# A decoder step on one core: the last feature pair of each chunk is split in two parts, and the end's pinned steps move one tile later

## The chip, the core and the metric

The kernel runs on one core of one Trainium2 chip. The metric is the device time of one execution in microseconds (us); a smaller time is better. The core has a matrix engine (TensorE, "PE" in the profile; its weight loads are "PEld"), a vector engine (VectorE, "DVE"), a scalar engine (ScalarE, "ACT"), GpSimd ("POOL") and SyncE ("SP"), which here only starts transfers. Each engine works through its own queue in order.

## What is computed

One step of a hybrid decoder trunk with model width 1024 on 520 tokens (512 new ones of a prompt and 8 single ones of a batch), all in float32:

```python
h = h + 0.5 * swiglu(rms_norm(h), ffn1)          # 1024 -> 2816 -> 1024
m = mixer(rms_norm(h))                           # pooling mixer + Mamba-2 mixer
h = h + m
h = h + 0.5 * swiglu(rms_norm(h), ffn2)          # 1024 -> 2816 -> 1024
y = rms_norm(h)
# swiglu(x) = (silu(x @ wg) * (x @ wu)) @ wd
```

The change touches the two feed-forward blocks (FFN1 and FFN2) and the last normalisation.

## The kernel before, in words

**Layout.** Features lie on the 128 partitions, tokens along the row. 520 tokens are two halves of 260 (`HALVES`); 2816 hidden features are 22 tiles of 128. A matrix product in nearly float32 precision is made of three matmuls (`mm3`, lines 121 to 126): each operand is split into a high part in a shorter format and the low remainder, and high x high (L122), high x low (L125) and low x high (L126) are added in one accumulator. So each operand needs a cast by ScalarE (the high part) and then a subtraction by VectorE (the low part).

**Seven products instead of eight.** The FFN class works on 2 x 2 blocks with a scheme of the Strassen-Winograd kind: `product` (L336) makes products number 1 to 7 of a step. Their left sides are sums of weight blocks, which `load` (L310) builds after the DMA (tiles `raw`, then `s`, `whi`, `wlo`, `shi`, `slo`); their right sides are seven sums of the activations, called slots 0 to 6, each with a high and a low part. For gate and up the slots of the normalised input lie in `xth` and `xtl`. For the down projection they are made of a *pair* of hidden features by `g_split` (L247): from the gated features `gx` (first of the pair) and `go` (second), each with two halves, it makes four differences `xd` (tile `gd` in the profile: L257, L258, L259, L261), and from these seven operands `x` the tile `gt`: slots 0 to 6 hold the high parts (casts on ScalarE, L265), slots 7 to 13 the low parts (subtractions on VectorE, L266). The tile's slot 0 is `gx[0]`, 1 is `go[0]`, 2 is `go[1]`, 3 to 6 are `xd[0]` to `xd[3]`. Only `go[0]` and `xd[3]` need the half that the closing product 4 gives.

**Order of a step.** `step` (L426) makes product 1 of step k, then product 4 of the step before, which was left pending (`flush`, L400), then products 5, 6, 3, 7, 2 of k, and then `gates` (L368), which on VectorE and ScalarE makes SiLU and the second half of the gated feature (`up(k, 1, ...)`, L383). `close` (L389) makes its first half (`up(k, 0, ...)`, L394) from product 4 and then calls `g_split` (L395).

**Chunks.** The 22 feature tiles fall into chunks of 6, 6, 6 and 4 (`CHUNKS`, L34). `rest` (L406) makes the steps of a chunk, then the first step of the next chunk, and then four down steps (c, 0), (c, 2), (c, 4), (c, 6), each with two tiles of the model width. So the last pair of a chunk closes in the first step of the next chunk, and the down step (c, 0) comes right behind that step. A down step reads three pairs, of which the last one (features 5, 11, 17) is the youngest. There are three such places in each FFN, six in all. The last chunk has no pairs and goes through `down` in FFN1 and `down_by_half` (L471) in FFN2. In the profile the down steps of FFN1 have the tiles `A1d`, `BE1d`, those of FFN2 `A2d`, `BE2d`.

**Who sets the order.** The tile framework's scheduler places the instructions of each engine by its own timeline, with the order of the program text as priority; where `keep_in_program_order` is called, instructions stay in that order among each other ("pinned").

**The end.** `down_by_half` makes for each half of the tokens the eight output tiles d = 0 to 7: twelve matmuls, an addition into `h` (L504), then `after2` (L611): a square on ScalarE, its sum on VectorE (L155), and a scaled copy into `hg` (L629). When tile 0 of the second half is reached, the sum of the first half is complete: `finish(0, ...)` (L631) puts the matmul with ones, two square roots on ScalarE (L639) and a list `todo` of six pinned steps on record: two reciprocals of 130 (L642) and four multiplications that give two output tiles each (L646), each followed by its DMA (L648, on SP's queue). `after2` takes one step of `todo` off per tile of the second half from d = 3 on (L615). With d = 7, `finish(1, ...)` adds the six steps of the second half, and all that is left is made.

Of the kernel before, what the change touches and what calls it, by code (L numbers as in the profile page):

```python
# [9 lines left out]
F32 = mybir.dt.float32  # L10
F32R = mybir.dt.float32r
AF = mybir.ActivationFunctionType
ALU = mybir.AluOpType
# [3 lines left out]
P = 128  # L17
# [4 lines left out]
HB = NT // 2  # L22
# [39 lines left out]
def tile_trunk_step(ctx: ExitStack, tc: tile.TileContext, ins: dict, outs: dict):  # L62
    nc = tc.nc
# [18 lines left out]
    def v(name, i, n=P):  # L82
        return vec[:n, VEC[name] + i : VEC[name] + i + 1]
# [37 lines left out]
    def mm3(ps, whi, wlo, xhi, xlo, start, stop, pin=False, **kw):  # L121
        first = nc.tensor.matmul(ps, whi, xhi, start=start, stop=False, **kw)  # L122
        if pin:
            tc.keep_in_program_order(first)
        nc.tensor.matmul(ps, whi, xlo, start=False, stop=False, **kw)  # L125
        nc.tensor.matmul(ps, wlo, xhi, start=False, stop=stop, **kw)  # L126

    def ws(w, k, m=P):
        return w[:, k * m : (k + 1) * m]
# [18 lines left out]
    def sumsq(acc, d, hs, name):  # L148
        n = hs.stop - hs.start
        if d == 0:  # L150
            nc.scalar.activation(out=acc[:, hs], in_=h[:, d, hs], func=AF.Square)
        else:
            sq = tmp.tile([P, HB], F32, tag="ta", name=f"sq_{name}_{d}")
            nc.scalar.activation(out=sq[:, :n], in_=h[:, d, hs], func=AF.Square)
            nc.vector.tensor_tensor(out=acc[:, hs], in0=acc[:, hs], in1=sq[:, :n], op=ALU.add)  # L155
# [48 lines left out]
    class Ffn:  # L204
# [39 lines left out]
            nc.scalar.copy(g[:, 0], t)  # L244
            nc.vector.tensor_tensor(out=g[:, 1], in0=t, in1=g[:, 0].bitcast(F32), op=ALU.subtract)

        def g_split(self, f):  # L247
            role = self.role(f)
            if role == "plain":
                self.g_plain(f, self.out[f])  # L250
            if role != "second":
                return
            gx, go = self.gx, self.out[f]
            self.gx = None
            t = self.gt[f] = self.gp.tile([P, 14, HB], F32R, tag="gt", bufs=3, name=f"gt{self.i}_{f}")
            xd = self.gp.tile([P, 4, HB], F32, tag="xd", name=f"gd{self.i}_{f}")
            nc.vector.tensor_tensor(out=xd[:, 0], in0=gx[:, 0], in1=gx[:, 1], op=ALU.subtract)  # L257
            nc.vector.tensor_tensor(out=xd[:, 1], in0=go[:, 1], in1=gx[:, 1], op=ALU.subtract)  # L258
            nc.vector.scalar_tensor_tensor(out=xd[:, 2], in0=xd[:, 1], scalar=-1.0, in1=gx[:, 0], op0=ALU.mult,  # L259
                                           op1=ALU.subtract)  # L260
            nc.vector.scalar_tensor_tensor(out=xd[:, 3], in0=xd[:, 2], scalar=-1.0, in1=go[:, 0], op0=ALU.mult,  # L261
                                           op1=ALU.subtract)
            for x, q in ((gx[:, 0], 0), (go, slice(1, 3)), (xd, slice(3, 7))):
                hi, lo = t[:, 0:7][:, q], t[:, 7:14][:, q]
                nc.scalar.copy(hi, x)  # L265
                nc.vector.tensor_tensor(out=lo, in0=x, in1=hi.bitcast(F32), op=ALU.subtract)  # L266

        def plain_load(self, f, j=None):
            if f not in self.raw:
                self.raw[f] = raw_pair(f"{self.i}_{f}")  # L270
            src = ins[f"w{self.i}gu"]
            for u in range(2):
                if j is None:
                    nc.sync.dma_start(out=self.raw[f][:, u], in_=src[2 * f + u])
                    continue
                q = (t.rearrange("p (q c) -> p q c", q=2)[:, :, j * P : j * P + P]
                     for t in (self.raw[f][:, u], src[2 * f + u]))
                nc.sync.dma_start(out=next(q), in_=next(q))
# [57 lines left out]
        def product(self, k, p):  # L336
            if k not in self.A:
                with tc.issue_after(self.behind[k]) if k in self.behind else nullcontext():
                    self.load(k)
                n = f"{self.i}_{k}" if not isinstance(k, tuple) else f"{self.i}d{k[1]}_{k[0]}"  # L340
                self.A[k] = ps[0].tile([P, 512], F32, tag="A", bufs=2, name=f"A{n}")
                self.BE[k] = ps[0].tile([P, 2, 512], F32, tag="BE", bufs=2, name=f"BE{n}")
                self.ac[k] = [self.wx.tile([P, 2, HB], F32, tag="ac", bufs=3, name=f"ac{n}_{q}") for q in range(2)]
            slot, dst, opens = {1: (0, 0, True), 2: (1, 1, True), 5: (3, 2, True), 6: (5, 0, False),
                                3: (2, 2, False), 7: (4, 0, False), 4: (6, 0, False)}[p]
            out = self.A[k] if dst == 0 else self.BE[k][:, dst - 1]
            (whi, wlo), k0 = self.w[k][p]
            xth, xtl = self.nx[:2]
            n = len(self.chunks[k[0]]) // 2 if isinstance(k, tuple) else KD // 2
            for j in range(n):  # L350
                if isinstance(k, tuple):
                    t = self.gt[self.chunks[k[0]][2 * j + 1]]
                    xhi, xlo = t[:, slot], t[:, 7 + slot]
                else:
                    xhi, xlo = xth[:, j, slot], xtl[:, j, slot]
                mm3(out[:, :HB], ws(whi, k0 + j), ws(wlo, k0 + j), xhi, xlo, opens and j == 0,
                    j == n - 1, skip_group_check=True)
            a, c = self.ac[k]
            keep = {1: a[:, 0], 6: a[:, 1], 7: c[:, 0], 5: c[:, 1]}.get(p)
            if keep is not None:  # L360
                nc.scalar.copy(keep, out[:, :HB])  # L361
            if p == 7:
                nc.vector.tensor_tensor(out=c[:, 0], in0=c[:, 0], in1=c[:, 1], op=ALU.add)
# [4 lines left out]
        def gates(self, k):  # L368
            n = f"{self.i}_{k}" if not isinstance(k, tuple) else f"{self.i}d{k[1]}_{k[0]}"
            r = self.nx[3].rearrange("p (b t) -> p b t", b=2)  # L370
            tg = self.tg[k] = self.wx.tile([P, 2, HB], F32, tag="tg", bufs=2, name=f"tg{n}")
            a, c = self.ac[k]
            nc.vector.tensor_tensor(out=tg, in0=self.BE[k][:, :, :HB], in1=a, op=ALU.add)  # L373
            if isinstance(k, tuple):
                hd, hn = h[:, k[1]], h[:, k[1] + 1, HALVES[1]]
                nc.vector.tensor_tensor(out=hd, in0=hd, in1=tg.rearrange("p b t -> p (b t)"), op=ALU.add)
                nc.vector.tensor_tensor(out=hn, in0=hn, in1=c[:, 0], op=ALU.subtract)
                return
            nc.vector.tensor_tensor(out=tg, in0=tg, in1=r, op=ALU.mult)  # L379
            nc.scalar.activation(out=tg, in_=tg, func=AF.Silu)  # L380
            self.g_homes(k)
            nc.vector.tensor_tensor(out=tg, in0=tg, in1=r, op=ALU.mult)  # L382
            self.up(k, 1, c[:, 0])  # L383

        def up(self, k, b, u):
            out, tg = self.out[k][:, b], self.tg[k][:, b]
            nc.vector.scalar_tensor_tensor(out=out, in0=u, scalar=-0.5, in1=tg, op0=ALU.mult, op1=ALU.mult)

        def close(self, k):  # L389
            if isinstance(k, tuple):  # L390
                hn = h[:, k[1] + 1, HALVES[0]]
                nc.vector.tensor_tensor(out=hn, in0=hn, in1=self.A[k][:, :HB], op=ALU.subtract)
                return
            self.up(k, 0, self.A[k][:, :HB])  # L394
            self.g_split(k)  # L395

        def scales(self):
            rstds(self.nx, f"f{self.i}")
# [125 lines left out]
    for j in range(KD // 2):  # L524
        for d in (j, j + KD // 2):
            q = slice(NVEC + d * NT if d else 0, NVEC + (d + 1) * NT)
# [82 lines left out]
    todo, late = [], []  # L609

    def after2(d, b, hs):  # L611
        hg, _, last = res
        if (d, b) == (0, 1):
            finish(0, [last[:, HALVES[0]]])
        elif b and todo and d > 2:  # L615
            todo.pop(0)()
        if b and d >= KD - 2:
            late.append(tmp.tile([P, HB], F32, tag="ta", name=f"sq_last{d}"))
            nc.scalar.activation(out=late[-1], in_=h[:, d, hs], func=AF.Square)
        else:  # L620
            sumsq(last, d, hs, f"l{d}{b}")
        if (d, b) == (KD - 1, 1):
            nc.vector.tensor_scalar(out=hg[:, d, hs], in0=h[:, d, hs], scalar1=v("final_norm", d), scalar2=None,
                                    op0=ALU.mult)
            finish(1, [last[:, hs], *late])
            while todo:
                todo.pop(0)()
            return
        nc.scalar.activation(out=hg[:, d, hs], in_=h[:, d, hs], func=AF.Copy, scale=v("final_norm", d))  # L629
# [585 lines left out]
```

## Time and profile before

| what | value |
|---|---|
| three timed runs | 992.83, 993.07 and 990.26 us; median 992.83 us |
| the profiled execution | 992.07 us, of which 990.3 us are the span of its instructions |
| mean granted TensorE clock in it | 0.996 of full speed |
| moved by DMA | 145.46 MB, mean 147 GB/s |

FFN1 lies from the start to about 360 us, the mixer to about 625 us, FFN2 from there to the end. All times of the trace count from the start of the span. In a timeline row the first number is the start, the second the duration of an instruction, then come engine, line, operation, what it writes and reads, and in brackets the idle time of the engine before it and what ended that. Because the engines are pipelined, an instruction starts a little before the one ahead of it has ended; the distance from start to start is what it takes of the queue.

### The profile page before, as it was taken

What the parts mean: (1) busy time and instruction counts of PE and PEld (TensorE: products, weight loads), DVE (VectorE), ACT (ScalarE), POOL (GpSimd) and SP (SyncE); (2) the same over time, 40 slices, a digit from 0 to 9 for tenths busy, and PEclk for the clock granted to TensorE, in tenths of its full rate; (3) what the DMA queues carried; (4) which work ended last, traced back from release to release, by engine and by line L of the source; (5) the groups of instructions that cost most, each with busy time, mean ns of one, the idle gap of its engine ahead of it and who ended that gap; (6) DMA issues with size and microseconds to landing.
All of it is one profiled execution on the core that took longest, in us unless ns stands there. A gap on an engine that the chain in (4) does not pass through costs nothing.

```text
span 990.3 us, 20220 instructions
## 1 busy us (share of the span) xinstructions
PE 955.2 (96%) x7636; PEld 929.3 (94%) x7636; DVE 877.1 (89%) x1612; ACT 677.7 (68%) x1251; POOL 218.2 (22%) x319
## 2 busy tenths in 40 slices
PE   7999999999999999999999999999999999999995
PEld 6899999999999999999899998899999989998995
DVE  7998999889989698788979987999989988997976
ACT  7676777677767565684755335678788878886864
POOL 0111211121122000167311000122332333323300
PEclk9999999999999999999999999999999999999999
DMA  5565765577566343263334322457688668776732
GB/s 183 157 170 110 191 163 141 131 184 180 116 153 159 75 140 114 89 222 106 105 120 136 136 82 88 117 148 181 147 219 202 154 166 223 169 174 156 193 87 87
DMA packets 63570, 145.46 MB, mean 147 GB/s; under 512 B 9256, under 2 KB 22504, under 8 KB 63472
## 3 DMA queue, kind: packets, MB, share of 16 engines
q1 hardware_dynamic: 41168, 103.78, 32.8%
q0 software_dynamic: 22304, 40.38, 22.4%
q8 instruction: 60, 0.98, 0.4%
q14 instruction: 38, 0.31, 0.1%
HBM read 136.80 MB, written 7.34 MB: 146 GB/s over the span
## 4 chain that ended last, share of the span: by engine, by line
PE 80%; DVE 11%; ACT 3%; issue 3%; POOL 1%; DMA 1%; SPq 0%; DVEq 0%; ACTq 0%
PE A L126 7%; PE A L122 7%; PE A L125 7%; PE BE L122 5%; PE BE L125 5%; PE BE L126 5%; PE P L292 3%; PE wo L122 2%; PE wo L126 2%; PE wo L125 2%; PE inz L122 2%; PE A1d L126 2%; PE A1d L122 2%; PE A1d L125 2%; PE inz L126 2%
## 5 line engine op out<-in xcount | busy, mean ns | idle before, releaser
L361 ACT COPY ac<-A 128x260 f32<-128x260 f32 x123 | 45.3, 370 | 16.6 <-PE A L126 16.3
L327 DVE TENSOR_TENSOR s<-raw 128x1024 f32<-128x1024 f32 x41 | 49.9, 1216 | 3.7 <-DMA raw<-in_w2gu 3.5
L292 PE MATMUL P<-xg_f,raw 128*128 128x260 f32 x192 | 45.9, 397 | 5.2 <-DMA raw<-in_w1gu 5.2
L292 PEld LDWEIGHTS P<-xg_f,raw 128*128 128x128 f32 x192 | 37.4, 198 | 11.4 <-ACT xg_f L188 5.2
L125 PE MATMUL wo<-catg,whi_wo 128*128 128x260 f32 x128 | 36.4, 285 | 1.3 <-DVE catg L1072 1.3
L923 POOL DMA_DIRECT2D out_nss<-hs x32 | 21.2, 663 | 74.4 <-DVE hs L941 69.2
L122 PE MATMUL wo<-catg,whi_wo 128*128 128x260 f32 x128 | 37.3, 292 | 0.3 <-DVE h L1041 0.3
L106 ACT CAST whi_wo<-raw_wo 128x1024 fp32r<-128x1024 f32 x12 | 12.5, 1045 | 36.5 <-issue 9.2
L122 PE MATMUL inz<-xh_mx,whi_inz 128*128 128x260 f32 x128 | 36.8, 287 | 0.0
L122 PE MATMUL inx<-xh_mx,whi_inx 128*128 128x260 f32 x128 | 36.4, 284 | 0.0
L126 PE MATMUL wo<-catg,wlo_wo 128*128 128x260 f32 x128 | 36.4, 284 | 0.0
L126 PE MATMUL inz<-xh_mx,wlo_inz 128*128 128x260 f32 x128 | 36.2, 283 | 0.0
L126 PE MATMUL inx<-xh_mx,wlo_inx 128*128 128x260 f32 x128 | 36.2, 283 | 0.0
L125 PE MATMUL inz<-xl_mx,whi_inz 128*128 128x260 f32 x128 | 36.1, 282 | 0.0
L125 PE MATMUL inx<-xl_mx,whi_inx 128*128 128x260 f32 x128 | 36.1, 282 | 0.0
L373 DVE TENSOR_TENSOR tg<-BE,ac 128x520 f32<-128x520 f32 x41 | 28.3, 691 | 5.2 <-PE BE L126 5.2
L787 DVE SCALAR_TENSOR_TENSOR A<-U,h,A 128x544 f32<-128x544 f32 x36 | 28.0, 778 | 4.2 <-ACT A L785 3.3
L382 DVE TENSOR_TENSOR tg<-tg,r_f 128x520 f32<-128x520 f32 x41 | 28.4, 693 | 1.2 <-ACT tg L380 0.9
L379 DVE TENSOR_TENSOR tg<-tg,r_f 128x520 f32<-128x520 f32 x41 | 28.4, 692 | 0.1
L329 DVE TENSOR_TENSOR s<-s,raw 128x512 f32<-128x512 f32 x41 | 28.0, 682 | 0.0
L328 DVE TENSOR_TENSOR s<-s,raw 128x512 f32<-128x512 f32 x41 | 28.0, 682 | 0.0
L380 ACT ACTIVATE tg<-tg 128x520 f32<-128x520 f32 x41 | 26.1, 638 | 1.2 <-DVE tg L379 1.2
(1787 smaller groups left out, 4748.8 us busy)
## 6 DMA issues: line engine op xcount, KB each, us to landing
raw<-in_w2gu SPq DMA_DIRECT2D x44, 512.0 KB, 4.9
raw<-in_w1gu SPq DMA_DIRECT2D x42, 512.0 KB, 4.7
raw_1d<-in_w1d SPq DMA_DIRECT2D x24, 384.0 KB, 3.9
raw_2d<-in_w2d SPq DMA_DIRECT2D x24, 384.0 KB, 4.0
raw_wo<-in_w_out SPq DMA_DIRECT2D x12, 512.0 KB, 4.5
ab<-scr_acs SPq DMA_DIRECT2D x8, 512.0 KB, 4.5
h<-in_state_ssm SPq DMA_DIRECT2D x16, 256.0 KB, 3.9
raw_inz<-in_w_in SPq DMA_DIRECT2D x8, 512.0 KB, 3.7
```

The source lines that it names most:

```text
L122: first = nc.tensor.matmul(ps, whi, xhi, start=start, stop=False, **kw)
L125: nc.tensor.matmul(ps, whi, xlo, start=False, stop=False, **kw)
L126: nc.tensor.matmul(ps, wlo, xhi, start=False, stop=stop, **kw)
L292: nc.tensor.matmul(self.banks[f, u][b][:, :HB], ws(self.raw[f][:, u], j + 4 * q), xg[:, slot[q]], start=j == q == 0, stop=j == 3 and q == ...
L327: nc.vector.tensor_tensor(out=s1, in0=diag, in1=up0, op=ALU.add)
L328: nc.vector.tensor_tensor(out=s2[:, 0], in0=s1[:, 1], in1=raw[:, 0, :nb], op=ALU.add)
L329: nc.vector.tensor_tensor(out=s2[:, 1], in0=s2[:, 0], in1=raw[:, 0, nb : 2 * nb], op=ALU.add)
L361: nc.scalar.copy(keep, out[:, :HB])
L373: nc.vector.tensor_tensor(out=tg, in0=self.BE[k][:, :, :HB], in1=a, op=ALU.add)
L379: nc.vector.tensor_tensor(out=tg, in0=tg, in1=r, op=ALU.mult)
L382: nc.vector.tensor_tensor(out=tg, in0=tg, in1=r, op=ALU.mult)
L787: nc.vector.scalar_tensor_tensor(out=A[:, :n], in0=U[:, j : j + n], scalar=w(j), in1=A[:, :n], op0=ALU.mult, op1=ALU.add)
```

## The change

`g_split` gets an argument `late`. It is now called twice for the *last* pair of a chunk: `gates` calls it with `late=False`, and then it makes the two tiles, `xd[0]`, `xd[1]`, `xd[2]` and the high and low parts of slots 0, 2 and 3 to 5; `close` calls it with `late=True`, and then it makes `xd[3]` and slots 1 and 6. For a last pair the cast and subtraction of 520 columns (slots 1 and 2) become two of 260 each, and those of 1040 columns (slots 3 to 6) become one of 780 (slots 3 to 5) and one of 260 (slot 6). Other pairs and the plain features are made as before, with `xd[3]` after the parts of slot 0 in the text. In the end, `d > 2` becomes `d > 3`.

```diff
-        def g_split(self, f):
+        def g_split(self, f, late=None):
             role = self.role(f)
-            if role == "plain":
+            if role == "plain" and late is not False:
                 self.g_plain(f, self.out[f])
             if role != "second":
                 return
+            last = f == self.chunks[self.chunk[f]][-1]
+            if not last and late is False:
+                return
             gx, go = self.gx, self.out[f]
-            self.gx = None
-            t = self.gt[f] = self.gp.tile([P, 14, HB], F32R, tag="gt", bufs=3, name=f"gt{self.i}_{f}")
-            xd = self.gp.tile([P, 4, HB], F32, tag="xd", name=f"gd{self.i}_{f}")
-            nc.vector.tensor_tensor(out=xd[:, 0], in0=gx[:, 0], in1=gx[:, 1], op=ALU.subtract)
-            nc.vector.tensor_tensor(out=xd[:, 1], in0=go[:, 1], in1=gx[:, 1], op=ALU.subtract)
-            nc.vector.scalar_tensor_tensor(out=xd[:, 2], in0=xd[:, 1], scalar=-1.0, in1=gx[:, 0], op0=ALU.mult,
-                                           op1=ALU.subtract)
-            nc.vector.scalar_tensor_tensor(out=xd[:, 3], in0=xd[:, 2], scalar=-1.0, in1=go[:, 0], op0=ALU.mult,
-                                           op1=ALU.subtract)
-            for x, q in ((gx[:, 0], 0), (go, slice(1, 3)), (xd, slice(3, 7))):
+            if not last or late is not True:
+                self.gt[f] = (self.gp.tile([P, 14, HB], F32R, tag="gt", bufs=3, name=f"gt{self.i}_{f}"),
+                              self.gp.tile([P, 4, HB], F32, tag="xd", name=f"gd{self.i}_{f}"))
+            t, xd = self.gt[f]
+
+            def low(x, q):
                 hi, lo = t[:, 0:7][:, q], t[:, 7:14][:, q]
                 nc.scalar.copy(hi, x)
                 nc.vector.tensor_tensor(out=lo, in0=x, in1=hi.bitcast(F32), op=ALU.subtract)
+
+            if not last or late is not True:
+                nc.vector.tensor_tensor(out=xd[:, 0], in0=gx[:, 0], in1=gx[:, 1], op=ALU.subtract)
+                nc.vector.tensor_tensor(out=xd[:, 1], in0=go[:, 1], in1=gx[:, 1], op=ALU.subtract)
+                nc.vector.scalar_tensor_tensor(out=xd[:, 2], in0=xd[:, 1], scalar=-1.0, in1=gx[:, 0], op0=ALU.mult,
+                                               op1=ALU.subtract)
+                low(gx[:, 0], 0)
+                if last:
+                    low(go[:, 1], 2)
+                    low(xd[:, 0:3], slice(3, 6))
+            if last and late is False:
+                return
+            nc.vector.scalar_tensor_tensor(out=xd[:, 3], in0=xd[:, 2], scalar=-1.0, in1=go[:, 0], op0=ALU.mult,
+                                           op1=ALU.subtract)
+            if last:
+                low(go[:, 0], 1)
+                low(xd[:, 3], 6)
+            else:
+                low(go, slice(1, 3))
+                low(xd, slice(3, 7))
...
             self.up(k, 1, c[:, 0])
+            self.g_split(k, False)
...
             self.up(k, 0, self.A[k][:, :HB])
-            self.g_split(k)
+            self.g_split(k, True)
...
-        elif b and todo and d > 2:
+        elif b and todo and d > 3:
```

More of the change, by code (lines that the diff above doesn't have):

```diff
@@ L351, in product @@
                 if isinstance(k, tuple):
-                    t = self.gt[self.chunks[k[0]][2 * j + 1]]
+                    t = self.gt[self.chunks[k[0]][2 * j + 1]][0]
                     xhi, xlo = t[:, slot], t[:, 7 + slot]
```

## The prediction

> **What bounds the kernel now.** First the page: span and busy shares. Then a row of the windows view from a step of FFN2. Then the waits of PE, to see what its few holes hang on, and at each hole the timelines of PE, DVE and ACT.
>
> ```profile
> span 990.3 us, 20220 instructions
> ...
> PE 955.2 (96%) x7636; PEld 929.3 (94%) x7636; DVE 877.1 (89%) x1612; ACT 677.7 (68%) x1251; POOL 218.2 (22%) x319
> ```
>
> ```profile
> 770.00:780.00 10.00, 10.00 (x86) 10.00 (x84) 10.00 (x19) 8.21 (x17) 3.42 (x6) 1.00 0.74 178
> ```
>
> TensorE is busy 96% of the span; inside a step it makes 86 matmuls in 10 us, 0.12 us each, without a hole (the first pair of the row; the third pair is DVE). So time is won only where PE waits. Its waits, each row with total, count and longest:
>
> ```profile
> PE BE2d L122 <- ACT gt L265: 2.9, 2, 1.5
> ...
> PE psl L635 <- DVE acc_last L155: 1.6, 1, 1.6
> ...
> PE BE1d L122 <- ACT gt L265: 1.0, 1, 1.0
> PE BE1d L125 <- DVE gt L266: 1.0, 2, 0.5
> ```
>
> The rows with `gt` are the six places where a down step (c, 0) waits for the youngest pair: first for its cast (L265), then for its subtraction (L266). The `psl` row is the end. These are just the places that the change touches. I number the six sites S1 to S3 (FFN1, features 5, 11, 17) and S4 to S6 (FFN2).
>
> **How a site works: S1.** PE, then DVE, then ACT.
>
> ```profile
> 90.88 0.28 PE L126 MATMUL A1d<-gt,slo_1d_0d 128*128 128x260 f32 x1
> 92.19 0.39 PE L122 MATMUL BE1d<-gt,shi_1d_0c 128*128 128x260 f32 x1 [1.03 <-ACT gt L265]
> ...
> 94.13 0.35 PE L125 MATMUL BE1d<-gt,shi_1d_0c 128*128 128x260 f32 x1
> ...
> 95.11 0.39 PE L122 MATMUL BE1d<-gt,shi_1d_0d 128*128 128x260 f32 x1 [0.29 <-ACT ac1d L361]
> ```
> ```profile
> 90.25 0.42 DVE L363 TENSOR_TENSOR ac<-ac 128x260 f32<-128x260 f32 x1
> 90.59 0.69 DVE L382 TENSOR_TENSOR tg<-tg,r_f 128x520 f32<-128x520 f32 x1
> ...
> 92.81 1.22 DVE L266 TENSOR_TENSOR gt<-gd,gt 128x1040 fp32r<-128x1040 f32 x1
> 93.96 0.54 DVE L329 TENSOR_TENSOR s_1d<-s_1d,raw_1d 128x384 f32<-128x384 f32 x1
> ```
> ```profile
> 87.83 0.37 ACT L361 COPY ac<-A 128x260 f32<-128x260 f32 x1
> ...
> 90.34 0.84 ACT L106 CAST whi_1d_0a<-raw_1d 128x768 fp32r<-128x768 f32 x1 [0.56 <-PE A L125]
> 91.09 1.05 ACT L265 CAST gt<-gd 128x1040 fp32r<-128x1040 f32 x1
> ```
>
> PE has nothing left from 90.88 + 0.12 on. The cast of 1040 stands behind a weight cast that itself waits for PE; it ends at 92.14. Then DVE has to reach the subtraction; it ends at 94.03. PE fills part of that time with nine matmuls of the next step's product 1 (9 x 0.12 = 1.08 us). Product 3 starts at 95.11.
>
> **The change, part by part.**
>
> *What it moves.* In the built order of the changed kernel the first part is not issued earlier: on DVE the gate's last product (L387 on `ac`) and the closing one (L387 on `A`) still follow each other directly, and the first difference and slot 0 stand where they stood. What changes is the width: the 780 columns of slots 3 to 5, which products 5, 6 and 7 need, no longer wait for `xd[3]`. Their cast moves on ACT ahead of that weight cast (S1, S5, S6), ahead of another one (S4), or stays where it was (S2, S3). Their subtraction moves on DVE to the place right behind L363 (S1 to S3), behind the first state addition (L941) and L261 (S5, S6), or behind L327 (S4). On PE the nine matmuls of product 1 at S1, S5 and S6 move behind products 3, 2 and 7. SP's order is the same; on POOL a few issues of the second halves of weights and of state tiles change places in FFN2.
>
> *What it adds.* Two DVE and two ACT instructions at each site, twelve of each. A 260-wide one takes 0.34 us of the DVE queue (90.25 to 90.59), the 1040-wide 1.15 (92.81 to 93.96), so a column costs 0.81/780 = 1.04 ns and each instruction has 0.34 - 0.27 = 0.07 us of its own. Twelve times 0.07 are 0.8 us of DVE, beside PE's work; if that cover is gone they cost 0.8 us.
>
> [...]
>
> *S1.* The new 780-wide subtraction starts where L382 started, later by 0.07 for the split 520: 90.66. Its length is known:
>
> ```profile
> L202 DVE TENSOR_TENSOR xtl_f<-xg_f,xth_f 128x780 fp32r<-128x780 f32 x8 | 7.7, 964 | 0.0
> ```
>
> It ends at 91.62 instead of 94.03. Its cast comes behind the copy at 87.83 and is done by 89.0, when PE is not there yet. PE does the high part and seven others until 91.23, waits to 91.68 (0.06 for the semaphore, as at S2 below), and product 3 follows 1.03 after that (S2's distance, 185.35 to 186.38): 92.71. Product 1's 1.08 us come later: gain 95.11 - 92.71 - 1.08 = **1.32 us**. The 0.28 of waiting for the copy (L361) stays.
>
> *S2 and S3.* Here the cast was early and the subtraction follows L363 already:
>
> ```profile
> 184.06 1.23 DVE L266 TENSOR_TENSOR gt<-gd,gt 128x1040 fp32r<-128x1040 f32 x1
> ```
> ```profile
> 185.35 0.39 PE L125 MATMUL BE1d<-gt,shi_1d_1c 128*128 128x260 f32 x1 [0.48 <-DVE gt L266]
> ...
> 186.38 0.39 PE L122 MATMUL BE1d<-gt,shi_1d_1d 128*128 128x260 f32 x1 [0.28 <-ACT ac1d L361]
> ```
>
> It ends 1.23 - 0.96 - 0.07 = 0.20 earlier: **0.20 us** each.
>
> *S5 and S6.*
>
> ```profile
> 796.35 0.28 PE L126 MATMUL A2d<-gt,slo_2d_1d 128*128 128x260 f32 x1
> 798.08 0.39 PE L122 MATMUL BE2d<-gt,shi_2d_1c 128*128 128x260 f32 x1 [1.45 <-ACT gt L265]
> ...
> 801.23 0.39 PE L122 MATMUL BE2d<-gt,shi_2d_1d 128*128 128x260 f32 x1 [0.28 <-ACT ac2d L361]
> ```
> ```profile
> 796.70 0.69 DVE L382 TENSOR_TENSOR tg<-tg,r_f 128x520 f32<-128x520 f32 x1
> ...
> 798.92 1.23 DVE L266 TENSOR_TENSOR gt<-gd,gt 128x1040 fp32r<-128x1040 f32 x1
> ```
>
> The subtraction takes L382's place here too: it starts at 796.70 + 0.07 and ends at 797.73; PE goes on at 797.79, product 3 at 798.82. Gain 801.23 - 798.82 - 1.08 = **1.33 us** each.
>
> *S6 has more.* Its hole is S5's, yet it lasts longer, because TensorE's clock falls:
>
> ```profile
> 891.27 0.28 PE L126 MATMUL A2d<-gt,slo_2d_2d 128*128 128x260 f32 x1
> ...
> 897.25 0.39 PE L122 MATMUL BE2d<-gt,shi_2d_2d 128*128 128x260 f32 x1
> ```
> ```profile
> 894.20:895.20 1.00, 1.00 (x5) 1.00 (x6) 1.00 (x2) 0.00 (x0) 0.10 (x1) 0.50 1.01 165
> ```
>
> From 796.35 to 801.23 are 4.88 us, from 891.27 to 897.25 are 5.98: the half clock (0.50, third value from the end) costs **1.10 us**. With a hole of 1.1 us in place of 1.6 and 0.6 I take it to stay away. It can be anything from 0 (the clock falls here as before, or at another site) to 2.2 (runs of before in which it fell at S5 too).
>
> [...] One fall in the changed kernel would make 987.4 of the forecast; I give it 2 in 10 of the forecast's chance, and it lies in its range.
>
> *S4.* Product 3 of (0, 0) waits for ACT's copy of product 5:
>
> ```profile
> 702.40 1.05 ACT L265 CAST gt<-gd 128x1040 fp32r<-128x1040 f32 x1
> 703.36 0.36 ACT L361 COPY ac2d<-A2d 128x260 f32<-128x260 f32 x1
> ...
> 705.76 0.38 ACT L361 COPY ac2d<-BE2d 128x260 f32<-128x260 f32 x1 [0.35 <-PE BE2d L126]
> ```
>
> ACT stood ready 0.35 before the copy, and PE was late because of the subtraction. That one now follows L327, four instructions earlier, so the 0.35 go. ACT itself wins the difference of a 1040-wide and a 260-wide cast, 0.96 - 0.27 = 0.69, less what the next weight cast then waits for PE; I take 0.15 of it. Gain **0.5 us**; bounds 0 (ACT comes no earlier) and 1.0 (0.35 and all of 0.69).
>
> *The end.*
>
> ```profile
> 974.76 0.97 DVE L642 RECIPROCAL r_last<-r_last 128x130 f32<-128x130 f32 x1 [1.66 <-ACT r_last L639]
> 975.64 0.37 DVE L504 TENSOR_TENSOR h<-dh,h 128x260 f32<-128x260 f32 x1
> ...
> 978.02 0.42 DVE L504 TENSOR_TENSOR h<-dh,h 128x260 f32<-128x260 f32 x1
> 978.36 0.69 DVE L646 TENSOR_TENSOR hg<-hg,r_last 128x520 f32<-128x520 f32 x1
> ...
> 979.30 0.42 DVE L504 TENSOR_TENSOR h<-dh,h 128x260 f32<-128x260 f32 x1
> ...
> 981.46 1.79 DVE L642 RECIPROCAL r_last<-r_last 128x130 f32<-128x130 f32 x2 [0.26 <-ACT r_last L639]
> ```
>
> The first reciprocal waits for ACT, and tile 4's addition stands behind it although its matmuls are done. One step later that addition falls into the idle 1.66, and one multiplication less (0.69, of which 0.08 overlap: 0.61) stands ahead of the last addition. From 974.76 the queue is two reciprocals (0.88 each), four additions (0.34 each) and one multiplication (0.61): the last addition at 978.48 instead of 979.30. Behind it come three multiplications (1.83) in place of two and the scaled copy (0.26) before the last reciprocals, at 978.48 + 0.34 + 2.09 = 980.91 instead of 981.46. ACT, which released them before, is earlier by 0.82 with the addition, so DVE holds them now. Gain **0.55 us**; none if the last outputs wait for their DMA instead.
>
> *Sum.* 1.32 + 2 x 0.20 + 0.50 + 2 x 1.33 + 1.10 + 0.55 = 6.5 us. Against the profiled execution that is 992.07 - 6.5 = 985.6 (its span of 990.3 and 1.8 around it); the median of the runs stands 0.76 higher, so 992.83 - 6.5 = **986.3 us**.
>
> **The rivals.** A measurement of this kernel tells about 0.3% (3 us) from no change.
>
> *A. VectorE gives it back in FFN2.* What PE gains there counts only if DVE keeps up. For it: in the row at 770 us DVE is as full as PE, 10.00 of 10. Against it: DVE too leaves the sites S5 and S6 earlier, since its next work waits for weight buffers that PE sets free. If all of S4 to S6 is lost: 992.83 - 1.32 - 0.40 - 0.55 = 990.6 us.
>
> *B. The filler loses its cover (slower).* At S1, S5 and S6 the nine matmuls used to run between high and low part. They now come later. If the 780-wide subtraction ends no earlier than the 1040-wide one did, the hole stays and 3 x 1.08 = 3.2 us are added, with 0.8 us of DVE and less 0.55 at the end: 992.83 + 3.5 = 996.3 us. It decides from an end of the subtraction at 91.6 + 1.3 = 92.9 (S1) or 799.1 (S5) on. Against it: nothing that stands ahead of it in the new queue waits for PE.
>
> *C. The change doesn't do what it says.* The part named for the gates is in fact issued where it was. If PE hangs on DVE's queue everywhere as at S2, each site gives 0.20: 992.83 - 1.2 - 0.55 = 991.1 us.
>
> **How the numbers follow.** The forecast has 0.68; A 0.14, B 0.08, C 0.10. The forecast's own range is 984.6 to 988.5: down by 1.1 for a second fall of the clock in before and by 0.6 for S4 (its bounds), up by 2.2 if the clock falls all the same (1.1), S4 gives nothing (0.5) and one site gives half (0.7). The range over the cases is 984.6 to 991.3; it leaves out B and little else. Faster by over 0.3% means under 989.9: the forecast, and a part of A in which only half is given back, 0.72. Within 0.3%: the rest of A, and C, 0.20. Slower: B, 0.08.
>
> **What would show it.** In the changed profile: no wait of PE for the cast of `gt` over 0.2 us; the wait for its subtraction some 0.4 at S1 to S3 and 1.1 at S5 and S6; product 3 at S1 and S5 without the nine matmuls ahead of it; no half clock near S6; the end's last addition under 1 us behind PE's last matmul. Wrong would make it: new waits of PE in FFN2 steps for weights (`slo`, `wlo`) of over 2 us together (A), waits for the subtraction of 2 us and more (B), or the 780-wide cast still behind a weight cast that waits for PE (C).

## The result and the profile after

| | before | after |
|---|---|---|
| median of 4 runs | 991.89 us (990.26 to 993.07) | 984.48 us (984.26 to 984.87) |
| ratio of the runs, 95% interval | | 0.9927 [0.991, 0.9944] |
| profiled execution, its span | 992.07 us, 990.3 us | 984.47 us, 982.6 us |

The changed kernel is faster by 7.4 us of median and 7.7 us of span. The forecast was 986.3 us, with 984.6 to 988.5 as its own range, so the measured median lies 0.1 us below that range. The kernel before has a fourth run here, 990.96 us, which brings its median from 992.83 down to 991.89; from that median the forecast 6.5 us less would be 985.4 us.

First the page of the changed kernel, the rows that answer to the ones shown of before:

```profile
span 982.6 us, 20242 instructions
...
PE 951.5 (97%) x7636; PEld 927.4 (94%) x7636; DVE 877.8 (89%) x1624; ACT 678.2 (69%) x1263; POOL 217.9 (22%) x319
```

The twelve added instructions of VectorE are there (1612 to 1624); its busy time has grown by 0.7 us. The waits of PE in FFN2 and the end, from 690 to 976 us (engine, line, what it waits for; total, times, longest):

```profile
PE BE2d L125 <- DVE gt L265: 1.7, 2, 0.9
PE BE2d L122 <- ACT ac2d L380: 1.3, 3, 0.7
PE BE L122 <- ACT ac L380: 0.3, 1, 0.3
PE psl L655 <- ACT sq_last L639: 0.2, 1, 0.2
```

The longest rows of before are gone: no wait for the cast of `gt` at a site (1.5 us) and no wait of `psl` for `acc_last` (1.6 us). What is left at S5 and S6 is the subtraction (now line L265) and ScalarE's copy (L380). Now the sites themselves, S1 on PE, DVE and ACT:

```profile
91.70 0.28 PE L122 MATMUL A1d<-gt,shi_1d_0d 128*128 128x260 f32 x1
92.26 0.39 PE L125 MATMUL BE1d<-gt,shi_1d_0c 128*128 128x260 f32 x1 [0.28 <-DVE gt L265]
...
93.29 0.39 PE L122 MATMUL BE1d<-gt,shi_1d_0d 128*128 128x260 f32 x1 [0.28 <-ACT ac1d L380]
```
```profile
90.90 0.43 DVE L382 TENSOR_TENSOR ac<-ac 128x260 f32<-128x260 f32 x1
91.24 0.97 DVE L265 TENSOR_TENSOR gt<-gd,gt 128x780 fp32r<-128x780 f32 x1
92.12 0.70 DVE L401 TENSOR_TENSOR tg<-tg,r_f 128x520 f32<-128x520 f32 x1
```
```profile
88.69 0.85 ACT L264 CAST gt<-gd 128x780 fp32r<-128x780 f32 x1
...
90.94 0.84 ACT L106 CAST whi_1d_0a<-raw_1d 128x768 fp32r<-128x768 f32 x1 [0.49 <-PE A L125]
```

The 780-wide cast stands ahead of the weight cast that waits for PE, the subtraction stands right behind the 260-wide `ac` sum, and PE waits 92.26 - 91.70 - 0.12 = 0.44 us for the subtraction alone, where before it waited for the cast and then, behind the nine matmuls of product 1, for the subtraction. Product 3 starts at 93.29. TensorE had started 0.59 us later in this execution, so that this is 92.70 on the clock of before; forecast was 92.71.

S5 and S6 on PE:

```profile
794.76 0.28 PE L122 MATMUL A2d<-gt,shi_2d_1d 128*128 128x260 f32 x1
795.89 0.39 PE L125 MATMUL BE2d<-gt,shi_2d_1c 128*128 128x260 f32 x1 [0.85 <-DVE gt L265]
...
796.92 0.39 PE L122 MATMUL BE2d<-gt,shi_2d_1d 128*128 128x260 f32 x1 [0.28 <-ACT ac2d L380]
```
```profile
888.56 0.39 PE L125 MATMUL BE2d<-gt,shi_2d_2c 128*128 128x260 f32 x1 [0.86 <-DVE gt L265]
...
889.59 0.39 PE L122 MATMUL BE2d<-gt,shi_2d_2d 128*128 128x260 f32 x1 [0.28 <-ACT ac2d L380]
```
```profile
888.00:889.00 1.00, 0.44 (x3) 0.44 (x4) 1.00 (x3) 0.65 (x2) 1.00 (x3) 1.00 0.42 162
889.00:890.00 1.00, 0.72 (x6) 0.51 (x5) 1.00 (x3) 0.65 (x2) 0.59 (x1) 1.00 0.49 149
```

S6 is now like S5, and the granted clock (third value from the end) stays at 1.00 where it was 0.50.

At S4 it is ScalarE's copy of product 5 that counts:

```profile
703.77 0.35 ACT L380 COPY ac2d<-BE2d 128x260 f32<-128x260 f32 x1
```

No idle time stands before it any more (0.35 us before, at 705.76). It comes 1.99 us earlier, of which 1.47 us are the lead that TensorE had before S4, so 0.52 us are won here: the 0.35 us that the prediction read off, and 0.17 us for which it had assumed 0.15.

To see where the 7.7 us come from, I followed TensorE's lead: both kernels have 7636 matmuls, in the same order but for the sites, so the start of the n-th one can be compared (before minus after). The last pair that counts so, the last matmul of the down projection, before and after:

```profile
977.54 0.28 PE L126 MATMUL dh<-gt,dlo_2d 128*128 128x260 f32 x1
```
```profile
970.59 0.28 PE L126 MATMUL dh<-gt,dlo_2d 128*128 128x260 f32 x1
```

| behind | at (before, us) | lead (us) | won there |
|---|---|---|---|
| start-up | 85 | -0.59 | -0.59 |
| S1, and the step behind it | 100, 150 | 0.79, 1.03 | 1.38 + 0.24 |
| S2, S3 | 195, 290 | 1.23, 1.42 | 0.20, 0.19 |
| the mixer | 690 | 1.45 | 0.03 |
| S4 | 715, 790 | 1.96, 1.89 | 0.51, -0.07 |
| S5, and the steps behind it | 803, 812, 830 | 3.23, 3.59, 4.14 | 1.34 + 0.36 + 0.55 |
| S6, and the step behind it | 899, 905, 976 | 6.59, 6.97, 6.95 | 2.45 + 0.38 - 0.02 |
| the end | span | 7.7 | 0.72 |

### The profile page after: what moved, and what is told of

Same layout as the page of the kernel before. It is cut to its first block, busy times and chain, and to the rows that moved or that the text cites. A ratio compares the mean times of both kernels' runs of the same rounds, so it can differ in the third digit from the quotient of the medians.

```text
span 982.6 us, 20242 instructions
## 1 busy us (share of the span) xinstructions
PE 951.5 (97%) x7636; PEld 927.4 (94%) x7636; DVE 877.8 (89%) x1624; ACT 678.2 (69%) x1263; POOL 217.9 (22%) x319
## 4 chain that ended last, share of the span: by engine, by line
PE 85%; DVE 8%; ACT 3%; issue 2%; DMA 1%; POOL 1%; SPq 0%; DVEq 0%; ACTq 0%
PE A L126 7%; PE A L122 7%; PE A L125 7%; PE BE L122 6%; PE BE L125 6%; PE BE L126 6%; PE P L311 3%; PE wo L122 2%; PE wo L125 2%; PE wo L126 2%; PE inz L122 2%; PE A2d L125 2%; PE A2d L126 2%; PE A1d L125 2%; PE A1d L126 2%
## 5 line engine op out<-in xcount | busy, mean ns | idle before, releaser
L380 ACT COPY ac<-A 128x260 f32<-128x260 f32 x123 | 45.1, 369 | 16.8 <-PE A L126 16.5
```

## The experiments

**The theories.** *Width* (the prediction's): the gain is that the 780 columns of slots 3 to 5 have a cast and a subtraction of their own, which need not wait for `xd[3]` and the closing product. *Place*: it is that a part is made by the call behind the gates at all. Beside them: what the end is worth, what the clock does, and what twelve more instructions cost. The medians of the kernel before in the three groups of runs are 992.79, 992.54 and 992.55 us (27, 10 and 11 runs).

**1. The pair part alone** (the end as before):

```diff
-        elif b and todo and d > 3:
+        elif b and todo and d > 2:
```

> The pair part alone: the two calls of g_split as in the changed kernel, the end as before (d > 2). The changed kernel measured 7.4 us under the kernel before, and its trace shows 6.7 to 7.0 us of that as a lead of TensorE at site S6 and 0.75 to 1.0 us at the end. My theory: the sites carry nearly all, so this gives 6.2 to 7.0 us less than the kernel before, about 985 us, with the waits at S1 to S6 as in the changed kernel (0.44 and 1.02 us for the subtraction). Rival: moving the pinned steps at the end is worth much more than the 0.55 us of the prediction; then this gives 5 us or less.

Measured: 984.86 us, ratio 0.9931 [0.9916, 0.9945]. That is 7.9 us by the medians, more than the 6.2 to 7.0 expected. In its trace TensorE has a lead of 6.42 us at the end, after a start-up 1.63 us behind, and the waits at the sites are those of the changed kernel; the mixer gave 0.5 us here and 0.03 in the changed kernel's trace, which no edit explains. The pair carries the change; the rival is out.

**2. The end alone:** the kernel before with

```diff
-        elif b and todo and d > 2:
+        elif b and todo and d > 3:
```

> The end alone: the kernel before with d > 3 in place of d > 2. My theory: the pair of reciprocals no longer stands ahead of tile 4's addition, and the last addition comes 0.8 us earlier: 0.5 to 1.0 us less than the kernel before, too little for the timed runs to tell but visible in the profile as the distance from TensorE's last matmul to the end of the span (the changed kernel has 0.75 to 1.0 us less of it than the kernel before). Rival: the last outputs wait for their DMA, and the distance stays: 0 us.

Measured: 991.67 us, ratio 0.9994 [0.9983, 1.0005]: too little for the timed runs, as expected. The waits of PE from 960 us on, and VectorE's last addition and last reciprocals:

```profile
PE psl L635 <- ACT sq_last L619: 0.2, 1, 0.2
```
```profile
978.27 0.42 DVE L504 TENSOR_TENSOR h<-dh,h 128x260 f32<-128x260 f32 x1
...
980.71 1.78 DVE L642 RECIPROCAL r_last<-r_last 128x130 f32<-128x130 f32 x2
```

The wait of 1.6 us for `acc_last` has become one of 0.2. TensorE's last matmuls (`psl`) come 1.05 us earlier than before, of which the last reciprocals (980.71 for 981.46) and the span (989.5 for 990.3) keep 0.8. The distance that was to show it, from the last matmul of the down projection to the end of the span, is 12.71 to 12.76 us in the five traces with the end as before and 12.02 to 12.06 us in the nine with the later steps. So the end is worth 0.7 us, here as in the changed kernel, and the rival is out.

**3. The place without the width.** The part behind the gates keeps slots 0 and 2, but slots 3 to 6 stay 1040 wide:

```diff
                     low(go[:, 1], 2)
-                    low(xd[:, 0:3], slice(3, 6))
...
-                low(xd[:, 3], 6)
+                low(xd, slice(3, 7))
...
-        elif b and todo and d > 3:
+        elif b and todo and d > 2:
```

> The place without the width, end as before: slots 0 and 2 of the last pair are still made by the call behind the gates, but slots 3 to 6 stay one cast and one subtraction of 1040 columns behind xd[3], in the call of close. So the same two calls, six more instructions each on VectorE and ScalarE, and no narrow subtraction. My theory: the width is what counts, so the six sites keep their waits (cast 1.0 to 1.5 us at S1, S5 and S6, subtraction about 0.5 us at S2 and S3) and the time is that of the kernel before within 1 us; a half clock near S6 is as likely as before. Rival: the early place of the first part is what counts (slot 2 and slot 0 ahead of the closing product); then this gets most of the 6 to 7 us.

Measured: 994.42 us, ratio 1.0027 [1.0011, 1.0042]: not the gain, and even slower. The place by itself wins nothing, so the rival is out; but my "within 1 us" was wrong too. (No run makes the narrow part in the call of `close`; what the width would give without the early call is not shown.) At S1, ACT and PE:

```profile
91.55 0.84 ACT L106 CAST whi_1d_0a<-raw_1d 128x768 fp32r<-128x768 f32 x1 [0.48 <-PE A L125]
92.29 0.51 ACT L109 ACTIVATE wlo_1d_0a<-raw_1d 128x384 fp32r<-128x384 f32 x1
92.71 1.04 ACT L264 CAST gt<-gd 128x1040 fp32r<-128x1040 f32 x1
```
```profile
93.81 0.39 PE L122 MATMUL BE1d<-gt,shi_1d_0c 128*128 128x260 f32 x1 [1.45 <-ACT gt L264]
...
95.83 0.39 PE L125 MATMUL BE1d<-gt,shi_1d_0c 128*128 128x260 f32 x1 [0.28 <-DVE gt L265]
```

The added instructions push the 1040-wide cast one place further back, behind L109 (0.42 us). TensorE loses 0.54 us at S1 and 0.57 at S5 against before, and 0.06 at each of the others: 1.35 us at the sites. The rest of the 1.9 us in its trace is a start-up 1.2 us late, of which the mixer gave 0.65 back.

**4. The split in FFN1 only, and 11. in FFN2 only** (the end as before in both):

```diff
-            last = f == self.chunks[self.chunk[f]][-1]
+            last = f == self.chunks[self.chunk[f]][-1] and str(self.i) == "1"
```

(number 11 has `"2"` in place of `"1"`).

> The split for the last pairs of FFN1 only (sites S1 to S3); FFN2's last pairs and the end as before. My theory: 1.32 + 0.20 + 0.20 = 1.7 us less than the kernel before by the lead of TensorE at S3 in the trace, and S5 and S6 keep their holes of 4.9 us and, where the clock falls, 6.0 us. Rival: the start-up and FFN1 give nothing in the end because the mixer waits for something else (a transfer, GpSimd) and takes the lead back; then the lead is gone before S4 and the time is that of the kernel before. The difference to the first kernel of this group is FFN2's share: 4.3 us by the prediction, 5 to 5.5 us by the trace of the changed kernel.

> The split for the last pairs of FFN2 only (S4 to S6); FFN1's last pairs and the end as before. With the kernel that has FFN1's alone (2.2 us less than the kernel before) it must add up to the pair part (7.9 us less by the medians, 7.0 by the traces without the start-up). The prediction has 0.50 + 1.33 + 1.33 + 1.10 = 4.3 us; the trace of the changed kernel shows 0.49, 2.25 and 2.81: 5.5 us less than the kernel before, some 987 us. My theory: 5.5 us, since the shorter holes let VectorE get ahead, and two later waits of S5 and one of S6 go as well; no fall of the clock at S5 and S6. Rival: those later waits went because TensorE and VectorE were shifted by FFN1's gain; then this shows 4.3 us and the later waits are still there.

Measured: FFN1 alone 990.61 us, ratio 0.9983 [0.997, 0.9996]; FFN2 alone 986.92 us, ratio 0.9948 [0.9934, 0.9961]. That is 2.2 and 5.6 us less than before, together 7.8, against 7.9 for both at once: by the medians the shares add up, each with an interval of 1.3 us to both sides. In the trace of the first, TensorE wins 1.51 + 0.52 = 2.03 us up to S3 (the start-up cost 0.52), and the mixer does not take them back. But behind S4, FFN2 takes 1.1 us of the lead (1.65 to 0.53), in a wait for weights that before does not have:

```profile
PE A2d L126 <- DVE slo_2d_0d L113: 0.9, 1, 0.9
```

With this wait and one fall of the clock more than in before, the profiled execution, the slowest of twelve, ends 0.8 us behind before, so that FFN1's 2.2 us stand on the medians and not on this trace. In the trace of the second, TensorE wins 5.16 us from S4 on (0.26 to 5.42), of these 0.52 at S4, 2.26 at S5 and 2.82 at S6, and 0.44 are lost between S4 and S5. The later waits are gone although FFN1 gave no lead, so that my theory holds and its rival doesn't.

The first of the two kernels also shows the clock fall at both wide sites; here S5, with the granted clock third from the end:

```profile
798.00:799.00 1.00, 0.52 (x4) 0.47 (x4) 1.00 (x3) 0.00 (x0) 0.88 (x2) 1.00 0.57 57
799.00:800.00 1.00, 1.00 (x8) 1.00 (x7) 1.00 (x2) 0.00 (x0) 0.00 (x0) 0.58 0.99 196
800.00:801.00 1.00, 1.00 (x6) 0.93 (x5) 0.44 (x2) 0.10 (x1) 0.00 (x0) 0.50 0.64 211
801.00:802.00 1.00, 0.91 (x5) 0.68 (x4) 0.00 (x0) 0.83 (x3) 0.00 (x0) 0.50 0.06 12
802.00:803.00 1.00, 1.00 (x8) 1.00 (x8) 0.00 (x0) 0.00 (x0) 0.00 (x0) 0.72 0.00 0
```

The half clock lasts (0.42 + 0.50 + 0.50 + 0.28)/0.5 = 3.4 us, and TensorE's lead falls there from 0.53 to -0.65, by 1.18 us.

**5. and 6. Filling what is left.** The products of the down steps (c, 0) in another order, in the changed kernel:

```diff
-            for p in (2, 5, 6, 3, 7) if k == KF - 1 else (5, 6, 3, 7, 2):
+            for p in ((2, 5, 6, 3, 7) if k == KF - 1 else (5, 6, 2, 3, 7) if isinstance(k, tuple) and not k[1]
+                      else (5, 6, 3, 7, 2)):
```

(number 6 has (2, 5, 6, 3, 7) in place of (5, 6, 2, 3, 7)).

> The changed kernel, but the down steps (c, 0) make their products in the order 5, 6, 2, 3, 7 instead of 5, 6, 3, 7, 2. In the changed kernel product 3 of these steps waits for ScalarE's copy of product 5: 0.44 + 0.11 us at S1 to S3, S5 and S6 and 0.88 + 0.10 at S4. My theory: TensorE's holes at the sites are real losses, one for one, so product 2's nine matmuls (1.08 us), which need only slot 1, cover them: 5 x 0.55 + 0.98 = 3.7 us at most, 3 us by my reckoning, some 981.5 us. Rival: the holes are given back, because VectorE is as full as TensorE in FFN2 and because the step then waits for product 7 instead; the time stays within 1 us of the changed kernel's 984.5.

> The changed kernel with product 2 first of all in the down steps (c, 0): 2, 5, 6, 3, 7. Its nine matmuls then stand ahead of product 5, whose last pair waits for the 780-wide subtraction (0.44 us at S1 to S3, 1.02 us at S5 and S6), and not between 6 and 3. My theory: 3 x 0.44 + 2 x 1.02 = 3.4 us are covered, while the wait for ScalarE's copy stays: 981 us. Rival: the subtraction's place in VectorE's queue is set by the copies and sums that hang on TensorE, so it comes as much later as TensorE comes later, and nothing is won: 984.5 us.

Measured: 983.81 us, ratio 0.9913 [0.9899, 0.9927], and 985.90 us, ratio 0.9933 [0.992, 0.9947]; 3 us were expected of each and neither gave them. Number 5 at S1, PE and ACT:

```profile
93.47 0.39 PE L122 MATMUL BE1d<-gt,whi_1d_0a 128*128 128x260 f32 x1 [0.28 <-ACT ac1d L380]
```
```profile
93.04 0.38 ACT L380 COPY ac1d<-BE1d 128x260 f32<-128x260 f32 x1 [0.36 <-PE BE1d L126]
```

This is product 2 (weights `whi_1d_0a`), and it waits for the same copy as product 3 did: the order of products puts it into the other half of the tile `BE1d` that ScalarE reads. The filler hung on what it was to hide, so this run says nothing on my theory; the little lead that it shows came in the mixer (-0.29 to 0.55 between 450 and 500 us), not at a site.

Number 6 did cover the subtraction: its waits from 690 to 976 us are

```profile
PE BE2d L122 <- ACT ac2d L380: 1.2, 3, 0.5
PE A2d L126 <- DVE slo_2d_1d L113: 0.4, 1, 0.4
PE A2d L126 <- DVE slo_2d_0d L113: 0.4, 1, 0.4
PE A2d L126 <- DVE slo_2d_2d L113: 0.4, 1, 0.4
PE BE2d L122 <- ACT whi_2d_1a L106: 0.3, 1, 0.3
PE BE2d L122 <- ACT whi_2d_2a L106: 0.3, 1, 0.3
PE psl L655 <- ACT sq_last L639: 0.2, 1, 0.2
```

No row with `gt` is left, but five with weights have come, low parts by VectorE and casts by ScalarE. Against the changed kernel it wins 0.9 us up to S3 (0.23 to 1.13) and loses 2.6 in FFN2 (1.17 to -1.43). This is the mechanism of the prediction's rival A, which the change itself did not set off: in FFN2 a hole that is filled on TensorE can come back as a wait for weights.

**7. A narrower part still:** slots 3 and 5 in one of 520, slot 4 in one of 260.

```diff
-                    low(xd[:, 0:3], slice(3, 6))
+                    low(xd[:, 0:3:2], slice(3, 6, 2))
+                    low(xd[:, 1], 4)
```

> The changed kernel with the 780-wide cast and subtraction cut once more: slots 3 and 5, which products 5 and 6 need first, in one of 520, and slot 4 in one of 260 of its own. My theory is that the width of what products 5 and 6 wait for is what sets the hole: 260 columns x 1.04 ns = 0.27 us less at each of S1, S2, S3, S5 and S6, 1.3 us in all if the place in the queue stays, for six more instructions on each of the two engines (0.07 us of queue each). In the built order the slot 4 subtraction stands ahead of the 520-wide one, so that my theory gives next to nothing: 0.07 us later at each site, 984.5 to 985 us. Rival (the number of instructions counts more than their width): 1 us or more slower than the changed kernel.

Measured: 984.58 us, ratio 0.9928 [0.991, 0.9946]: nothing, as my theory had it. The 260 columns stay ahead in the queue, and at S1 TensorE wins 1.30 us in its trace where the changed kernel wins 1.38. Its six runs spread from 983.43 to 988.37 us, so the time alone could not tell 0.4 us.

**8. and 10. The price of the added instructions:** the split for every second feature but each FFN's first, twice.

```diff
-            last = f == self.chunks[self.chunk[f]][-1]
+            last = role == "second" and self.chunks[0][1] != f
```

> The changed kernel with the two-part split for all second features but the first one, which its six sites do not need: 20 more casts on ScalarE and 20 more subtractions on VectorE, 260 wide. This prices the added instructions by themselves. My theory: each takes 0.07 us of the queue, 1.4 us of VectorE, beside TensorE's work, so the time stays within 0.5 us of the changed kernel's 984.5. Rival A: VectorE is full in FFN2, so the queue time of ten of them comes back on TensorE there, 0.7 us. [...]

> The kernel with the split for all second features but each FFN's first, a second time, to settle on one chip whether it beats the changed kernel (983.5 us against 984.5 us measured apart). By its trace TensorE leads the changed kernel by 0.5 us at the end, of which the start-up gave 1.0 and FFN2 took 1.1 back between 715 and 750 us. My theory: the twenty added instructions cost nothing and win nothing either, so it is within 0.5 us of the changed kernel. Rival: narrower parts help at every pair; 1 us faster again.

Measured: 983.47 us, ratio 0.9911 [0.9896, 0.9925], and 984.80 us, ratio 0.9926 [0.9912, 0.994]. The page of the first:

```profile
PE 950.8 (97%) x7636; PEld 926.8 (94%) x7636; DVE 877.8 (89%) x1644; ACT 679.6 (69%) x1283; POOL 217.4 (22%) x319
```

Twenty instructions more (1644 for 1624), and VectorE is as busy as in the changed kernel. By the traces TensorE wins 7.0 and 7.5 us behind the start-up, the changed kernel 7.5 and 8.0; so there may be 0.5 us of cost, which the medians do not show (in FFN2 two waits of 0.43 us of the gate steps and one of 1.1 us for `slo` at 725 us are new). Rival A (0.7 us) can't be told from my theory. The second, measured together with number 9, is 0.4 us below it, so that "1 us faster" is not shown either. A subtraction of 260 columns lasts 0.42 us (the median of 18 in before, L266); a price per added instruction the medians here do not show.

**9. The changed kernel again:**

> The changed kernel itself once more, beside the kernel before and the next three on one chip. My theory of the clock: the holes of the six sites are now too short for it to fall, so its runs lie closely together (within 1 us but for the start-up) at 984 to 985.5 us, with a mean granted clock of 0.996 or more in every run, while those of the kernel before spread over 3 us and more with a clock down to 0.993. Rival: the narrow spread of the first four runs was chance, and one run in three shows a fall (1.1 us more, a clock of 0.994 or 0.995).

Measured: 985.24 us, ratio 0.9935 [0.9918, 0.9951]. Four of six runs lie at 984.1 to 985.4 us, two at 988.0 and 988.1, one of these with a mean clock of 0.994. My theory asked for every run to lie closely together with a clock of 0.996 or more, and so it did not hold. The rival is not shown either: the two runs are 3 us slower, not the 1.1 us of one fall, and only one of them has the clock of a fall. Of these two there is no trace, and what happened in them stays open. With the first four runs, eight of ten lie at 984.1 to 985.4 us.

**12. Numbers 5 and 8 together:**

> The split for all second features but each FFN's first, and products in the order 5, 6, 2, 3, 7 in the steps (c, 0): the two kernels that were fastest so far put together (983.5 and 983.8 us). The product order alone left TensorE's waits at the sites as they were (product 2 writes the tile BE that ScalarE's copy of product 5 reads, and its first matmul waits for the same copy), so I expect nothing from it: within 0.5 us of the kernel with the split alone. Rival: both small gains are real and add up to 982.8 us.

Measured: 983.63 us, ratio 0.9912 [0.9899, 0.9925]. It is the lowest of its group, but the interval overlaps with those of 9 and 10, and its trace has TensorE win 7.3 us behind the start-up, no more than the changed kernel. I do not call any of these versions faster than the changed kernel.

## Why the prediction was right

The mechanism held, and run 3 rules out the rival *Place*. The terms against the lead of TensorE:

| term | forecast | measured |
|---|---|---|
| S1 | 1.32 | 1.38, and 0.24 in the step behind it |
| S2, S3 | 0.20 each | 0.20, 0.19 |
| S4 | 0.50 | 0.51 |
| S5 | 1.33 | 1.34, and 0.91 in the steps behind it |
| S6, the half clock with it | 1.33 + 1.10 | 2.45, and 0.36 in the step behind it |
| the end | 0.55 | 0.72 |
| start-up, mixer, S4 to S5 | not named | -0.63 |
| sum | 6.5 | 7.7 |

At the sites themselves the forecast is right within 0.1 us. What makes 7.7 out of 6.5 is 1.5 us behind the sites and 0.2 at the end, less 0.6 at the start-up. So the sum was too small by 1.2 us; this and the lower median of before put the measured time just below the range. Two things were luck: the late start of this execution hid 0.6 us of what was missing, and at S4 the 0.15 us for ScalarE was chosen, not worked out.

**What was not in the sum: the waits behind the sites.** The prediction asked what is late next, and only looked for new waits. The old ones behind the sites are the larger matter: 0.24 + 0.91 + 0.36 = 1.5 us. Before, at 806.9 us, PE and ACT, and at 822.9 us, PE:

```profile
806.89 0.28 PE L126 MATMUL A2d<-gt,wlo_2d_1b 128*128 128x260 f32 x1
807.26 0.39 PE L122 MATMUL BE2d<-gt,shi_2d_1d 128*128 128x260 f32 x1
...
822.94 0.39 PE L126 MATMUL A2d<-gt,slo_2d_1d 128*128 128x260 f32 x1 [0.29 <-DVE slo_2d_1d L113]
```
```profile
806.55 0.40 ACT L940 ACTIVATE so<-br,sxdt 128x128 f32<-128x128 f32 x1
806.85 0.36 ACT L361 COPY ac2d<-BE2d 128x260 f32<-128x260 f32 x1
```

The copy of product 5 stands behind the state's work on ScalarE, and PE's product 3 (807.26) comes too early for it. The same step after, ACT and PE:

```profile
802.24 0.39 ACT L960 ACTIVATE so<-br,sxdt 128x128 f32<-128x128 f32 x1
...
802.79 0.37 ACT L380 COPY ac2d<-BE2d 128x260 f32<-128x260 f32 x1
```
```profile
802.79 0.28 PE L122 MATMUL A2d<-gt,whi_2d_1b 128*128 128x260 f32 x1
...
803.75 0.28 PE L122 MATMUL BE2d<-gt,shi_2d_1d 128*128 128x260 f32 x1
```

The copy starts 0.96 us ahead of product 3 instead of 0.41. That PE comes later relative to ScalarE because the nine matmuls (1.08 us) now lie between the site and this step is my reading; it was not tried apart. What is shown: this wait of product 3, 0.35 us with what follows it, stands behind S5 and S6 in all four traces with wide sites in FFN2 (before, 2, 3 and 4) and in none of the ten with the split there; the wait for `slo`, 0.5 to 0.8 us, stands behind S5 or S6 in each of those four, and of the ten only in number 6, which changed the order. Run 11 has lost both with FFN2's split alone. The wait for `slo` is not bound to the wide sites, though: behind S4 it came in 4, 6, 8 and 10 (0.3 to 1.1 us). In the three traces that have just the changed kernel's sites (after, 1 and 9) it stands at none of these places, so its 0.55 us belong to this kernel's gain; another kernel need not keep them.

**The clock.** The prediction gave 1.10 us for one fall and let it range from 0 to 2.2. Among the four traces with wide sites it fell at S6 in all and at S5 in one; in ten traces with the split in FFN2, at neither. In the group with 27 runs of the kernel before, two with a mean clock of 0.997 have a median of 989.85 us, ten with 0.996 have 992.17, and nine with 0.993 or 0.994 have 993.44. This fits a number of falls that differs from run to run, but these runs have no trace, and the mean clock alone does not tell (0.996 stands for one fall in before and for none in number 7; one run with 0.998 took 993.19 us). That a hole of 1.1 us keeps the clock up was my assumption, which no row of before showed; the ten traces agree with it at S5 and S6. A fall lasted 3.4 us at S6 of before (893.78 to 897.19) and at S5 and S6 of number 4.

**The end.** 0.55 was made of the last reciprocals: forecast 980.91, and they came, set back to before's clock, at 973.82 + 6.95 = 980.77. As the prediction said, the last addition lies under 1 us behind PE's last matmul of the down projection (970.59), and the reciprocals no longer wait for ACT:

```profile
971.39 0.42 DVE L524 TENSOR_TENSOR h<-dh,h 128x260 f32<-128x260 f32 x1
...
973.82 1.78 DVE L662 RECIPROCAL r_last<-r_last 128x130 f32<-128x130 f32 x2
```

**The rivals.** A: no wait for `slo` or `wlo` over 0.2 us in FFN2 of the changed kernel; but the mechanism exists, as runs 4, 6 and 8 show. B: the subtraction at S1 ended at 91.24 + 0.97 = 92.21, by before's clock 91.62, ahead of the point of 92.9. C: the sites give 1.3 us, not 0.20. The start-up was not thought of: it differs from execution to execution (TensorE 1.63 us later than before in run 1, 0.44 earlier in run 8), so that one trace against another is uncertain by that much.

## What to carry to other kernels

Where an operand is made in one wide instruction, look which of its columns are needed first and which input holds it back; a narrow one without the late input can move whole places forward in its queue (at S1 its subtraction started at 90.65 us by before's clock, not at 92.81), while an earlier call with the full width moved nothing forward here (run 3, 994.42 us). Price a hole with what follows it: small waits in the next steps went with it (1.5 us of 7.7), new ones took 1.1 us of the lead back in run 4, and where the clock fell in a hole, that cost another 1.1 to 1.2 us. Before work is moved into a hole, see whether it writes a tile that the awaited instruction reads (in run 5 product 2 waited 0.28 us for that).

## What the runs showed of the hardware

TensorE was not idle throughout ahead of a fall: counting 0.12 us per matmul, it stood still for 2.1 to 2.5 of the 3.4 us (the length of a fall) ahead of each of the five falls in FFN2, and for 1.7 us at most in any such stretch at S5 and S6 of the changed kernel, where no trace shows one. Three stretches with 2.5 us, S5 of before, 2 and 3, went without a fall, so it is not the length of the hole alone.

Where the hole lies on a fixed grid fits all eight holes. In before the trace's record of the granted clock starts at 9.73 us; the fall at 893.78 lies 884.05 = 259 x 3.4133 us behind that, the fall behind TensorE's last matmul, at 985.94, another 92.16 = 27 such steps. In the changed kernel the one fall, at 976.22, also behind the last matmul, lies 965.97 = 283 such steps behind the start of the record at 10.25. In 2 and 3 the two falls (893.56 and 982.30, 895.58 and 987.74 us) lie 26 and 27 steps apart, in number 4 the three (799.16, 894.72 and 986.88 us) 28 and 27. Counted in the steps of this grid, TensorE stood still for 2.1 to 2.5 us in the step ahead of each fall, and for at most 1.6, 1.7 and 2.0 us in any step at S5 of before, 2 and 3. So which of these like holes was hit goes with where the grid cut it. The border between 2.0 and 2.1 us rests on these eight holes and on 0.12 us per matmul; that S5 and S6 of the changed kernel have 1.7 us at most, wherever the grid lies, goes with the clock staying up there.

In this program two halves of one accumulator tile (`BE`, 512 values each) hold each other up: a matmul into one waited 0.28 us for ScalarE's copy of the other (93.47 in run 5). Whether the hardware or only the program's semaphores ask for it was not tried.
